# A hybrid attention block on one core: merged tiles split eight units after turning, an early table load, and a larger scratch for GpSimd's DMAs

## The chip, the core and the metric

The kernel runs on one core of a Trainium2 chip. The core has five engines with a queue each: TensorE (PE, matmuls; PEld is its weight loads), VectorE (DVE), ScalarE (ACT), GpSimd (POOL) and SyncE (SP, which here only issues DMAs). Each engine works through its own instructions in the order in which the program wrote them, and waits on semaphores for the others. The metric is device time of one execution in microseconds. The kernel before takes 912.95 us, the median of three runs (914.67, 907.07 and 912.95). Durations below come from one more execution, the profiled one: 913.56 us, of which 911.8 us are the span from the first to the last instruction.

## What is computed

One layer of a decoder block on 256 tokens of width 2048, in float32. The projections, cut to what matters here:

```python
h = rmsnorm(x, norm_w)
proj = h @ w_in            # u_pool, g_pool, q, kc_raw, vc_raw, k_sel, v_sel, k_win, v_win, g_nsa, g_br
y_pool = pool_mixer(u_pool, pool_mix, pool_scale) * silu(g_pool)
y_a = y_pool @ w_pool_out
# q, k with rope; compressed, selected and window attention, added with gates sigmoid(g_br)
y_b = (o_nsa * silu(g_nsa)) @ w_nsa_out
gm = sigmoid(h @ w_merge + b_merge).reshape(b, s, 2, D_MODEL)
merged = gm[:, :, 0] * y_a + gm[:, :, 1] * y_b
x = x + merged @ w_out
return rmsnorm(x, final_norm_w)
```

## The kernel before, in words

**Units.** The weights are cut into 314 units, in the order of `plan()`: `p` (pool inputs and gates of the branches, 420 or 416 columns), `mix`, `kc`, `vc`, `ks`, `kw`, `vs`, `vw` and the compression weights `w1k`, `w1v`, then four times `q`, `gn`, `m`, `po` (one for each group of four heads, called head 0 to 3 here), then `m4`, `m5`, `no0`, `no1`, `m6`, `no2`, `m7`, `no3` and `wo0` to `wo3`. Most are a chunk of eight units, each of 256 rows by 512 columns. The tile names carry the unit's number: `w260` is the raw weight, `h260` and `l260` its two parts.

**Three matmuls for one.** A float32 product is made of three matmuls in a rounded type: the high part `h` of the weight by the high part of the activations (L227), the low part `l` by the high part (L228), and `h` by the low part (L229). So every unit is loaded by SP, copied to `h` by ScalarE (L214), and VectorE subtracts `l = w - h` (L215). A unit is twelve matmuls: two blocks of 128 rows, two blocks of tokens, three products.

**The loop.** At step `s` the main loop writes the load of unit `s+6` (`load`), the split of unit `s+3` (`cut`), the matmuls of unit `s`, and then `advance()`, which takes one piece of work from each of five lanes (`e`, `a`, `c`, `d`, `b`). A lane is a queue of generators: the next generator begins only when the one before has ended, and each `yield` is one step. This is what sets the order of everything beside the weights. An engine may run ahead of TensorE, but not out of its own order.

**Turning.** Activations have to lie transposed for the next product. `turn` does this in lane `a` in two parts: VectorE transposes 32x32 blocks of both token blocks into `r` (STREAM_TRANSPOSE, L275, one for each token block, called the first and the second transpose here), and GpSimd then writes `r` to DRAM with one DMA (`W`, L280) and reads it back in four DMAs (L284), which put the blocks in place. The result is then split by ScalarE (`mh`, `qh`) and VectorE (`ml`, `ql`), after `TURN` = 4 further steps for `q` and for the merged tiles `m0`, `m1`, `m2` (the last, `m3`, is turned by TensorE), and after eight for `ks` and `kw`. The gates `gn` and `gp` are turned but not split.

**Merged tiles.** When chunk `no` `i` is done, `evac_no` multiplies it by its gate (VectorE, `gm`, L862), GpSimd adds it to `merged` (`mg`, L863), and `merge_t(i)` turns and splits it. The results are needed only by `wo`.

**Attention.** When `qT` of a head group is split, two generators `attend` follow in lane `b`: scores in PSUM (`S`, two buffers), added to a mask by VectorE (L702), the maxima (`mx`, L708 to L713), the exponentials by ScalarE (L723, with a load of its function table ahead of them where another function ran before), the weights, and the transposes by TensorE.

**The start.** Eight matmuls on zeros (`warm`) run while the first loads come. `x_piece(0)` brings in the first part of `x` in two halves, beside the two halves of unit 0; `cut(0)` makes unit 0's `h` on VectorE (L1078), half by half, with the parts `xh` (ScalarE, L217) and `xl` (VectorE, L218) of `x` in between.

Of the kernel before, what the change touches and what calls it, by code (L numbers as in the profile page):

```python
# [11 lines left out]
F32 = mybir.dt.float32  # L12
F32R = mybir.dt.float32r
BF16 = mybir.dt.bfloat16
AF = mybir.ActivationFunctionType
OP = mybir.AluOpType
# [172 lines left out]
def body(nc, tc, d, out):  # L189
# [7 lines left out]
    def blk(dt, name):  # L197
        return sb.tile([128, NB], dt, tag="B", bufs=NBLK, name=name)

    def half(dt, name):  # L200
        return sb.tile([128, 512], dt, tag="H", bufs=NHALF, name=name)
# [4 lines left out]
    def psum(tag, name):  # L206
        return pp.tile([128, 512], F32, tag=tag, bufs={"P": 4, "S": 2, "T": 2}[tag], name=name)

    mm, act, dve, pool = nc.tensor.matmul, nc.scalar.activation, nc.vector, nc.gpsimd

    def split(hi, lo, src, scale=None, eng=None):

        if scale is None:
            act(hi, src, AF.Copy)  # L214
            (eng or dve).tensor_tensor(lo, src, hi.bitcast(F32), op=OP.subtract)  # L215
        else:
            act(hi, src, AF.Copy, scale=scale)  # L217
            dve.scalar_tensor_tensor(lo, src, scale, hi.bitcast(F32), op0=OP.mult, op1=OP.subtract)  # L218
# [16 lines left out]
    def C(name):  # L235
        a, b = CONST[name]
        return ct[:, a:b]
# [32 lines left out]
    def turn(name, srcs, dst):  # L270


        r = blk(F32, name + "R")
        for tok, src in enumerate(srcs):
            dve.transpose(r[:, tok * 512:tok * 512 + 512].rearrange("p (b h j) -> p h b j", b=4, h=4),  # L275
                          src.rearrange("p (h b j) -> p h b j", h=4, b=4))
        yield

        w = dp.tile([128, 1024], F32, tag="W", bufs=NTURN, name=name + "W")
        pool.dma_start(w, r[:, :1024])  # L280
        wv = w.rearrange("(a i) (k b x) -> b i k a x", a=4, k=2, b=4)
        dv = dst[:, :1024].rearrange("p (k a x) -> p k a x", k=2, a=4)
        for b in range(4):
            pool.dma_start(dv[32 * b:32 * b + 32], wv[b])  # L284

    def by_head(g):

        return g[:, :1024].rearrange("p (c h j) -> p h c j", h=4, j=32)
# [4 lines left out]
    def x_piece(j):  # L293
        st = half(F32, f"xs{j}")
        if j == 0:

            nc.scalar.dma_start(nw, nwt)
            nc.scalar.dma_start(st[:, :256], xT[j][:, :256])
            unit_load(0, 0)
            nc.sync.dma_start(st[:, 256:], xT[j][:, 256:])  # L300
            unit_load(0, 1)
        else:
            nc.sync.dma_start(st, xT[j])
        if j % 2 == 0:
            xh.append(blk(F32R, f"xh{j}"))
            xl.append(blk(F32R, f"xl{j}"))
        return st

    def x_split(j, st, k):
        kt = 2 * j + k  # L310
        o = (kt % 4) * 256
        split(xh[kt // 4][:, o:o + 256], xl[kt // 4][:, o:o + 256], st[:, k * 256:k * 256 + 256],
              scale=nw[:, kt:kt + 1])
# [8 lines left out]
    def x_square(j, st):  # L322

        if j == 0:
            pool.memset(ones, 1.0)
            act(sq, st, AF.Square)
        else:
            act(st, st, AF.Square)
            pool.tensor_tensor(sq, sq, st, op=OP.add)

    def warm():

        z = half(BF16, "zero")
        dve.memset(z, 0.0)
        ps = psum("T", "warm")
        for _ in range(NWARM):
            mm(ps, z[:, :128], z, start=True, stop=True)
# [63 lines left out]
    def pool_load():  # L401
        bt.extend(blk(F32, f"bt{k}") for k in range(3))
        for k, w in enumerate((1024, 512, 1024)):
            nc.sync.dma_start(bt[k][:, :w], bic[k][:, :w])
# [35 lines left out]
    def pool_mix():  # L440
        yield
        for k in range(2):
            gpT.append(blk(F32, f"gpT{k}"))
            yield from turn(f"gp{k}", [gpn[tok][:, k * 512:k * 512 + 512] for tok in range(2)], gpT[k])
            yield
# [171 lines left out]
    def keys(kind, b, rot):  # L617
        yield
        g = blk(F32, f"{kind}T")
        yield from turn(kind, rot, g)  # L620
        for _ in range(2 * TURN):
            yield

        runs = [[KTt[h][:, z + 16 + b * 128:z + 400 + b * 128] for z in (0, 528)] for h in range(4)]
        split4([[runs_of(t) for t in pair] for pair in runs],
               [by_head(g)[:, h].rearrange("p (k a) j -> p k a j", k=2) for h in range(4)])
# [24 lines left out]
    def queries(i, rot):  # L651
        yield
        qTt[i] = (blk(F32R, f"qh{i}"), blk(F32R, f"ql{i}"))
        g = blk(F32, f"qT{i}")
        yield from turn(f"q{i}", rot, g)
        for _ in range(TURN):
            yield
        split(*(x[:, :1024].rearrange("p (h c j) -> p h c j", h=4, j=32) for x in qTt[i]), by_head(g))
        for pr in range(2):
            later("b", attend(i, pr))  # L660
# [196 lines left out]
    def evac_no(i, ps):  # L857
        g = gm.pop(4 + i)
        for tok in range(2):
            t = g[:, tok * 512:tok * 512 + 512]  # L860
            m = merged[tok, i // 2][:, (i % 2) * 512:(i % 2) * 512 + 512]
            dve.tensor_tensor(t, ps[tok], t, op=OP.mult)  # L862
            pool.tensor_tensor(m, m, t, op=OP.add)  # L863
            if tok == 0:
                yield
        later("a", merge_t(i))

    def merge_t(i):
        yield
        mh.append(blk(F32R, f"mh{i}"))  # L870
        ml.append(blk(F32R, f"ml{i}"))
        o = (i % 2) * 512
        if i == 3:

            for tok in range(2):
                pt = psum("T", f"mT{i}{tok}")
                for h in range(4):
                    nc.tensor.transpose(pt[:, h * 128:h * 128 + 128],
                                        merged[tok, 1][:, o + h * 128:o + h * 128 + 128], C("ident"))
                split(*(x[i][:, :1024].rearrange("p (h t) -> p h t", h=4)[:, :, tok * 128:tok * 128 + 128]  # L880
                        for x in (mh, ml)), pt.rearrange("p (h t) -> p h t", h=4))
                if tok == 0:
                    yield
            return
        g = blk(F32, f"mT{i}")
        yield from turn(f"m{i}", [merged[tok, i // 2][:, o:o + 512] for tok in range(2)], g)
        for _ in range(TURN):
            yield
        split(*(x[i][:, :1024].rearrange("p (h c j) -> p h c j", h=4, j=32) for x in (mh, ml)), by_head(g))

# [155 lines left out]
    def unit_load(s, k=None):  # L1046
        u = units[s]
        if s not in raw:
            raw[s] = blk(F32, f"w{s}")
        c = slice(0, u.n) if k is None else slice(k * u.n // 2, (k + 1) * u.n // 2)  # L1050
        nc.sync.dma_start(raw[s][:, c], wts[u.off:u.off + 128 * u.n].rearrange("(p n) -> p n", p=128)[:, c])

    def load(s):
        if s >= N:
            return
        if s < 16 and s % 2 == 0:
            xst[s] = x_piece(s // 2)
        if s:
            unit_load(s)
        if s == 24:  # L1060
            nc.sync.dma_start(ct, cst)
        if s == 18:
            pool_load()
        if units[s].pre:
            units[s].pre(units[s].i)

    def cut(s):
        if s >= N:
            return
        u = units[s]  # L1070
        h, l = blk(F32R, f"h{s}"), blk(F32R, f"l{s}")
        r = raw.pop(s)
        n = u.n // 2
        st = xst.pop(s, None)
        if s == 0:
            for k in range(2):
                o = slice(k * n, k * n + n)
                dve.tensor_copy(h[:, o], r[:, o])  # L1078
                x_split(0, st, k)
                dve.tensor_tensor(l[:, o], r[:, o], h[:, o].bitcast(F32), op=OP.subtract)  # L1080
        else:
            if st is not None:
                for k in range(2):
                    x_split(s // 2, st, k)
            split(h[:, :u.n], l[:, :u.n], r[:, :u.n])
        if s % 2 and s < 16:
            x_square(s // 2, xsq.pop())
        if st is not None:
            xsq.append(st)
        hl[s] = (h, l)  # L1090


    warm()
    loaded = cutted = 0
    for s in range(N):
# [27 lines left out]
TURN = 4  # L1123
# [2 lines left out]


def build():
    nc = bacc.Bacc("TRN2", target_bir_lowering=False, num_devices=1, dynamic_dma_scratch_size=1024)
    return nc  # L1130


# [35 lines left out]
```

## Time and profile before

| | |
|---|---|
| runs | 914.67, 907.07, 912.95 us; median 912.95 |
| profiled execution | 913.56 us, span 911.8 us |
| TensorE busy (modelled) | 892.4 us, 98% of the span |
| TensorE weight loads | 751.0 us, 82% |
| VectorE | 590.2 us, 65% |
| ScalarE | 461.9 us, 51% |
| GpSimd | 155.9 us, 17% |
| moved by DMA | 189.02 MB, 207 GB/s over the span |
| chain that ended last, by engine | PE 88%, DMA 4%, issue 3%, ACT 2%, DVE 2%, POOL 1% |

Reading: the ends of matmuls are modelled, so the busy time of TensorE says whether it had work, not how fast it was. How fast it was is read from the starts of neighbouring matmuls, from the count of matmuls in a stretch, and from the granted clock.

### The profile page before, as it was taken

To read this page: it belongs to the slowest core of one execution; us is meant where nothing else is said; L and a number is where in the kernel's file an instruction comes from. 1 tells how busy PE (TensorE), PEld (TensorE's weight loads), DVE (VectorE), ACT (ScalarE), POOL (GpSimd) and SP (SyncE) were. 2 spreads that over 40 slices of the span, in tenths; PEclk is the share of its full clock that TensorE was granted. 3 is DMA by queue.
4 is the path that set the end of the run, shared out by engine and by line. 5 is a ranking of instruction groups with operands and counts; after the bars stand their busy time and mean duration, and the time that the engine had idled before them with its cause. 6 is when DMAs were issued, how large, how long until landed. Compare 5 with 4: busy or idle time off the path is not lost.

```text
span 911.8 us, 11860 instructions
## 1 busy us (share of the span) xinstructions
PE 892.4 (98%) x4289; PEld 751.0 (82%) x4289; DVE 590.2 (65%) x889; ACT 461.9 (51%) x723; POOL 155.9 (17%) x145
## 2 busy tenths in 40 slices
PE   8999999999999999999999999999999979999996
PEld 7999988888888888887888888878888858888886
DVE  7756457877846476867686868576774526357633
ACT  6566545635634366456646655576562315246510
POOL 2203226333002110201021102010002311111110
PEclk9999999999999999999999999999999999999998
DMA  9955686788875664575556655666576674696602
GB/s 346 382 160 177 228 248 190 232 271 256 287 224 181 204 181 150 188 208 180 168 187 216 183 159 179 205 193 204 167 243 198 190 236 152 206 381 213 225 1 92
DMA packets 56154, 189.02 MB, mean 207 GB/s; under 512 B 6944, under 2 KB 7456, under 8 KB 56096
## 3 DMA queue, kind: packets, MB, share of 16 engines
q1 hardware_dynamic: 50768, 172.40, 58.8%
q0 software_dynamic: 5040, 15.73, 5.7%
q8 instruction: 33, 0.54, 0.2%
q14 instruction: 25, 0.20, 0.1%
q10 hardware_dynamic: 288, 0.14, 0.1%
HBM read 178.29 MB, written 9.96 MB: 206 GB/s over the span
## 4 chain that ended last, share of the span: by engine, by line
PE 88%; DMA 4%; issue 3%; ACT 2%; DVE 2%; POOL 1%; ACTq 0%; DVEq 0%; POOLq 0%
PE m L228 5%; PE m L229 5%; PE m L227 5%; PE p L227 3%; PE p L228 3%; PE p L229 3%; PE q L228 3%; PE wo L228 3%; PE wo L227 3%; PE wo L229 3%; PE q L229 3%; PE q L227 3%; PE gn L228 3%; PE gn L229 3%; PE gn L227 3%; PE no L228 3%
## 5 line engine op out<-in xcount | busy, mean ns | idle before, releaser
L215 DVE TENSOR_TENSOR l<-w,h 128x1024 fp32r<-128x1024 f32 (+2 forms) x313 | 386.0, 1262 | 80.6 <-ACT h L214 79.3
L214 ACT ACTIVATE h<-w 128x1024 fp32r<-128x1024 f32 (+2 forms) x313 | 308.2, 1030 | 56.5 <-DVE l L215 15.6
L227 PE MATMUL m<-h,xh 128*128 128x512 f32 x256 | 101.2, 395 | 0.0
L229 PE MATMUL m<-h,xl 128*128 128x512 f32 x256 | 100.8, 394 | 0.0
L228 PE MATMUL m<-l,xh 128*128 128x512 f32 x256 | 100.8, 394 | 0.0
L227 PE MATMUL p<-h,xh 128*128 128x420 f32 (+1 forms) x160 | 57.6, 360 | 1.4 <-ACT xh L217 1.4
L228 PE MATMUL p<-l,xh 128*128 128x420 f32 (+1 forms) x160 | 57.1, 357 | 0.6 <-DVE l L1080 0.6
L229 PE MATMUL p<-h,xl 128*128 128x420 f32 (+1 forms) x160 | 57.2, 357 | 0.0
L229 PEld LDWEIGHTS m<-h,xl 128*128 128x128 f32 x256 | 48.0, 188 | 11.1
L227 PEld LDWEIGHTS m<-h,xh 128*128 128x128 f32 x256 | 48.3, 189 | 9.9
L228 PEld LDWEIGHTS m<-l,xh 128*128 128x128 f32 x256 | 48.1, 188 | 9.8
L227 PE MATMUL no<-h,yh 128*128 128x512 f32 x128 | 51.6, 403 | 4.5 <-ACT h L214 4.5
L723 ACT ACTIVATE S<-S,mx 128x16 f32<-128x16 f32 (+2 forms) x96 | 37.7, 394 | 35.7 <-DVE mx L713 35.7
L227 PE MATMUL wo<-h,mh 128*128 128x512 f32 (+1 forms) x144 | 53.2, 369 | 0.0
L228 PE MATMUL wo<-l,mh 128*128 128x512 f32 (+1 forms) x144 | 53.1, 369 | 0.0
L229 PE MATMUL wo<-h,ml 128*128 128x512 f32 (+1 forms) x144 | 53.0, 368 | 0.0
L228 PE MATMUL no<-l,yh 128*128 128x512 f32 x128 | 51.5, 402 | 0.7 <-DVE l L215 0.7
L227 PE MATMUL gn<-h,xh 128*128 128x512 f32 x128 | 51.6, 403 | 0.0
L229 PE MATMUL no<-h,yl 128*128 128x512 f32 x128 | 51.4, 401 | 0.0
L227 PE MATMUL q<-h,xh 128*128 128x512 f32 x128 | 51.0, 398 | 0.0
L229 PE MATMUL gn<-h,xl 128*128 128x512 f32 x128 | 50.5, 395 | 0.0
L228 PE MATMUL q<-l,xh 128*128 128x512 f32 x128 | 50.5, 394 | 0.0
(336 smaller groups left out, 1768.6 us busy)
## 6 DMA issues: line engine op xcount, KB each, us to landing
w<-wts SPq DMA_DIRECT2D x274, 512.0 KB, 4.3
w<-wts SPq DMA_DIRECT2D x31, 420.0 KB, 7.3
w<-wts SPq DMA_DIRECT2D x8, 416.0 KB, 3.3
bb<-bmr SPq DMA_DIRECT2D x8, 256.0 KB, 4.9
xr<-xn SPq DMA_DIRECT2D x4, 512.0 KB, 6.8
out<-ot SPq DMA_DIRECT2D x8, 256.0 KB, 2.5
xs<-xT SPq DMA_DIRECT2D x7, 256.0 KB, 7.3
bt<-bic SPq DMA_DIRECT2D x2, 512.0 KB, 9.0
```

Of the source, the lines that this page charges most:

```text
L214: act(hi, src, AF.Copy)
L215: (eng or dve).tensor_tensor(lo, src, hi.bitcast(F32), op=OP.subtract)
L227: mm(o, ah, bh, start=start, stop=False)
L228: mm(o, ah, bl, start=False, stop=False)
L229: mm(o, al, bh, start=False, stop=stop)
L723: act(s, s, AF.Exp, bias=mx[:, k:k + 1], scale=SCALE, accum_out=sm[:, k:k + 1])
```

## The change

Five edits, all in the order of work:

1. `merge_t` waits `2 * TURN` = 8 steps between the turn and the split of the merged tiles, instead of 4.
2. In `turn`, the `yield` stands between the two transposes; the second transpose and the DMAs are written in the same step. The number of steps is the same. This holds for every turn (`gp`, `ks`, `kw`, `q`, `gn`, `m`).
3. ScalarE runs a one-element copy in `x_piece(0)` right behind its two DMA issues.
4. Units 0 and 1 are loaded in halves and split in halves; apart from the first half of unit 0, ScalarE makes their `h`. VectorE subtracts unit 0's first `l` before it makes `xl`.
5. The scratch memory of GpSimd's DMAs is 2048 instead of 1024.

```diff
         for tok, src in enumerate(srcs):
             dve.transpose(r[:, tok * 512:tok * 512 + 512].rearrange("p (b h j) -> p h b j", b=4, h=4),
                           src.rearrange("p (h b j) -> p h b j", h=4, b=4))
-        yield
+            if tok == 0:
+                yield
@@ x_piece(0)
             nc.scalar.dma_start(st[:, :256], xT[j][:, :256])
+
+            act(small(1, "tab"), zeros[0][:, :1], AF.Copy)
             unit_load(0, 0)
             nc.sync.dma_start(st[:, 256:], xT[j][:, 256:])
             unit_load(0, 1)
+            unit_load(1, 0)
+            unit_load(1, 1)
@@ merge_t
-        for _ in range(TURN):
+        for _ in range(2 * TURN):
             yield
@@ load
-        if s:
+        if s > 1:
             unit_load(s)
@@ cut
-        if s == 0:
+        if s < 2:
+
             for k in range(2):
                 o = slice(k * n, k * n + n)
-                dve.tensor_copy(h[:, o], r[:, o])
-                x_split(0, st, k)
-                dve.tensor_tensor(l[:, o], r[:, o], h[:, o].bitcast(F32), op=OP.subtract)
+                if s == 0 and k == 0:
+                    dve.tensor_copy(h[:, o], r[:, o])
+                else:
+                    act(h[:, o], r[:, o], AF.Copy)
+                if s == 0 and k == 0:
+                    dve.tensor_tensor(l[:, o], r[:, o], h[:, o].bitcast(F32), op=OP.subtract)
+                    for x in range(2):
+                        x_split(0, st, x)
+                else:
+                    dve.tensor_tensor(l[:, o], r[:, o], h[:, o].bitcast(F32), op=OP.subtract)
@@ build
-    nc = bacc.Bacc("TRN2", target_bir_lowering=False, num_devices=1, dynamic_dma_scratch_size=1024)
+    nc = bacc.Bacc("TRN2", target_bir_lowering=False, num_devices=1, dynamic_dma_scratch_size=2048)
```

What stands in the queues at three places. First ScalarE's queue at the start of the program, before (`xs` is a piece of `x`, `sq` its squares, `h` and `w` a unit):

```order
L298 DMA xs_93<-xT 128x256
L217 ACT_TABLE_LOAD
L217 ACTIVATE xh_100<-xs_93,nw 128x256 x2
L214 ACTIVATE h_132<-w_102 128x840
L326 ACTIVATE sq<-xs_93 128x512
```

and of the change:

```order
L299 DMA xs_93<-xT 128x256
L301 ACT_TABLE_LOAD
L301 ACTIVATE tab<-zero 128x1
L217 ACTIVATE xh_105<-xs_93,nw 128x256 x2
L1090 ACTIVATE h_125<-w_98 128x420
L1090 ACTIVATE h_135<-w_102 128x420 x2
L331 ACTIVATE sq<-xs_93 128x512
```

The table load now stands ahead of the copy `tab`, which needs no load, and the second half of unit 0 and both halves of unit 1 are ScalarE's. Second, ScalarE's queue around the split `mh1` of the second merged tile, before:

```order
L214 ACTIVATE h259_6583<-w259_6527 128x1024
L214 ACTIVATE mh1_6497<-mT1_6499 128x1024
L214 ACTIVATE h260_6603<-w260_6545 128x1024
L214 ACTIVATE h261_6623<-w261_6563 128x1024
L214 ACTIVATE h262_6644<-w262_6581 128x1024
```

and of the change:

```order
L214 ACTIVATE h265_6704<-w265_6645 128x1024
L214 ACTIVATE h266_6722<-w266_6664 128x1024
L214 ACTIVATE mh1_6556<-mT1_6558 128x1024
L214 ACTIVATE h267_6742<-w267_6682 128x1024
L214 ACTIVATE h268_6760<-w268_6700 128x1024
```

`mh1` moved from ahead of `h260` to ahead of `h267`, `mh0` from ahead of `h252` to ahead of `h256`, `mh2` from ahead of `h276` to ahead of `h280`. Because lane `a` is served in order, `merge_t(1)` begins only after `mh0`: VectorE's first transpose of `m1` now stands behind `l255`, `ml0`, `l256` and `l257` too, its second behind `l258`. Third, VectorE's queue at the turn of `q1` (`P`, `sm`, `Cn` and `S` belong to the attention of head group 0), before:

```order
L275 STREAM_TRANSPOSE q1R<-q1r0a 128x4x4x32
L275 STREAM_TRANSPOSE q1R<-q1r1a 128x4x4x32
L215 TENSOR_TENSOR P_3220<-p_3484,P_3220 128x2x128
L734 TENSOR_TENSOR sm_3365<-sm_3365,ct 128x1
L735 RECIPROCAL sm_3365<-sm_3365 128x6
L736 TENSOR_TENSOR sm_3365<-sm_3365,gates 128x6
L738 TENSOR_SCALAR Cn_3217<-S_3328,sm_3365 128x3x16
```

and of the change, up to the second transpose:

```order
L275 STREAM_TRANSPOSE q1R<-q1r0a 128x4x4x32
L215 TENSOR_TENSOR P_3225<-p_3488,P_3225 128x2x128
L742 TENSOR_TENSOR sm_3370<-sm_3370,ct 128x1
L743 RECIPROCAL sm_3370<-sm_3370 128x6
L744 TENSOR_TENSOR sm_3370<-sm_3370,gates 128x6
L746 TENSOR_SCALAR Cn_3222<-S_3333,sm_3370 128x3x16
L750 TENSOR_SCALAR S_3333<-S_3333,sm_3370 128x128 x2
L746 TENSOR_SCALAR Cn_3222<-S_3333,sm_3370 128x3x16
L750 TENSOR_SCALAR S_3333<-S_3333,sm_3370 128x2x128 x2
L215 TENSOR_TENSOR l_3505<-w_3408,h_3504 128x1024
L275 STREAM_TRANSPOSE q1R<-q1r1a 128x4x4x32
```

The second transpose of `q1`, and with it GpSimd's five DMAs, moved behind ten instructions; `q2` and `q3` read the same, at `q0` only one `l` lies between. The second transpose of `gn1` moved from ahead of the maxima `mx` to behind them and the next `l`.

## Rows read from the trace of the kernel before

**Rows 1.** Busy time by stretch: span part, engines busy (count), granted clock, DMA

```profile
core 0: us, PE busy (x) PEld busy (x) DVE busy (x) ACT busy (x) POOL busy (x), PEclk, DMA share, GB/s
0.00:20.00 20.00, 16.82 (x68) 13.68 (x69) 13.99 (x20) 13.63 (x23) 4.29 (x8) 0.91 0.92 339
...
400.00:420.00 20.00, 18.68 (x94) 15.48 (x93) 14.05 (x27) 13.03 (x32) 4.59 (x6) 1.00 0.76 237
...
580.00:600.00 20.00, 18.26 (x96) 15.15 (x95) 13.82 (x22) 13.96 (x25) 2.39 (x4) 1.00 0.72 220
...
740.00:760.00 20.00, 14.81 (x52) 11.20 (x52) 11.13 (x11) 11.11 (x12) 0.59 (x1) 0.83 0.40 129
...
780.00:800.00 20.00, 20.00 (x88) 16.28 (x87) 6.12 (x7) 4.79 (x5) 2.41 (x4) 1.00 0.68 199
```

**Rows 2.** Waits of TensorE: us in total, times, longest

```profile
PE no L227 <- ACT h L214: 4.5, 1, 4.5
PE S L227 <- DVE S L702: 3.1, 3, 1.5
PE p L227 <- ACT xh L217: 1.4, 1, 1.4
```

**Rows 3.** Timeline of the start: start, us, engine, line, operation [idle before <- releaser]

```profile
4.30 1.28 ACT L217 ACT_TABLE_LOAD   x1 [4.30 <-DMA xs<-xT]
...
6.16 0.46 PE L227 MATMUL p<-h,xh 128*128 128x420 f32 x1 [1.41 <-ACT xh L217]
...
7.04 0.37 DVE L1078 CAST h<-w 128x420 fp32r<-128x420 f32 x1
...
10.67 1.98 DVE L215 TENSOR_TENSOR l<-w,h 128x840 fp32r<-128x840 f32 x2 [0.28 <-ACT h L214]
...
13.24 0.35 PE L227 MATMUL p<-h,xh 128*128 128x420 f32 x1
```

**Rows 4.** Timeline, TensorE and ScalarE at the splits mh1 and mh2

```profile
743.97 0.40 PE L229 MATMUL no<-h,yl 128*128 128x512 f32 x1
...
746.85 1.06 ACT L214 ACTIVATE mh<-mT 128x1024 fp32r<-128x1024 f32 x1 [19.49 <-DMA mT<-m1W]
...
748.90 0.79 PE L227 MATMUL no<-h,yh 128*128 128x512 f32 x1 [4.53 <-ACT h L214]
...
755.58 0.39 PE L228 MATMUL no<-l,yh 128*128 128x512 f32 x1
...
793.17 1.06 ACT L214 ACTIVATE mh<-mT 128x1024 fp32r<-128x1024 f32 x1 [16.19 <-DMA mT<-m2W]
```

**Rows 5.** GpSimd's timeline at two turns, and all its reads back

```profile
386.44 1.82 POOL L284 DMA_DIRECT2D qT<-q1W  x3 [5.21 <-ACT h L214]
392.33 0.59 POOL L284 DMA_DIRECT2D qT<-q1W  x1 [4.07 <-issue]
...
735.66 1.82 POOL L284 DMA_DIRECT2D mT<-m1W  x3 [9.65 <-DMA m1W<-m1R]
741.63 0.59 POOL L284 DMA_DIRECT2D mT<-m1W  x1 [4.16 <-issue]
...
DMA to landing us min/median/max: 2.6/4.9/7.9
```

**Rows 6.** Timeline of VectorE and ScalarE from the turn of q1 to head 1

```profile
379.68 0.66 DVE L275 STREAM_TRANSPOSE q1R<-q1r1a 128x512 f32<-128x512 f32 x1
...
382.41 2.35 DVE L215 TENSOR_TENSOR l<-w,h 128x1024 fp32r<-128x1024 f32 x2
...
396.90 1.06 ACT L214 ACTIVATE qh<-qT 128x1024 fp32r<-128x1024 f32 x1 [4.01 <-DMA qT<-q1W]
...
405.56 1.30 DVE L275 STREAM_TRANSPOSE gn1R<-gn 128x512 f32<-128x512 f32 x2
...
409.05 1.28 ACT L723 ACT_TABLE_LOAD   x1 [0.96 <-DVE mx L713]
```

**Rows 7.** Busy time while q1 is read back, columns as in rows 1

```profile
392.00:396.00 4.00, 4.00 (x19) 3.27 (x18) 1.67 (x2) 0.88 (x1) 0.59 (x1) 1.00 0.81 212
```

## What the change will do to the time: a prediction

> **What bounds the kernel now.** I read the busy time by stretch first. TensorE has work all the time in almost every 20 us; a usual stretch holds 88 matmuls, 0.23 us from start to start (20 us / 88). Four stretches fall short: the start, 400 to 420, 580 to 600, and 740 to 760, where only 52 matmuls stand and the granted clock is 0.83 [rows 1]. So the end is set by TensorE, and time is won only where TensorE itself stands still or runs at the lower clock. Its waits then say for whom: once 4.5 us for a weight's high part `h`, three times (3.1 us together, at most 1.5) for VectorE's `S`, once 1.4 us at the start for `xh` [rows 2]. Each edit is judged by these places.
>
> **Edit 1, the later split of merged tiles.** At 746.85 ScalarE starts `mh1` after 19.49 us of standing idle for the read back of `m1`; `h260` is queued behind it, and TensorE, which has started its last matmul at 743.97, gets its next only at 748.90 [rows 4]. The wait costs more than its 4.5 us: from the matmul at 743.97 to the one at 755.58 there are 14 steps [rows 4]; at 0.23 us they take 3.2 us, and they took 11.6. The loss is 8.4 us, waits and half clock together (the clock of 0.83 over 20 us is 3.4 us of it [rows 1]).
>
> In the new order `mh1` stands ahead of `h267`. Without the stall TensorE comes to `h260` at 744.2 and, at twelve matmuls of 0.23 us a unit (2.76 us), to `h267` at 763.5. When is `m1` back? VectorE's transposes of `m1` come behind at most five more instructions of about 1.2 us (two `l` take 2.35 us [rows 6]), so `mh1` could start at 746.85 + 6.0 = 752.9 at the latest of what I can name, 10 us ahead of need. `mh2` must be ready for `h280`, at 744.2 + 20 x 2.76 = 799.4; before it started at 793.17 [rows 4], and its chain starts 8.4 us earlier, with TensorE's. `mh0` only gains room. So the wait has somewhere to go: ScalarE still idles, but with `h` for units ahead already made. **-8.4 us**; bounds 0 (the wait is only moved) and -8.4.
>
> **Edits 3 and 4, the start.** The first real matmul starts at 6.16, after `xh`, which waited for a table load of 1.28 us that ScalarE began only when its data was there, at 4.30 [rows 3]. Until then ScalarE does nothing but issue two DMAs, so a load put there is covered, and `xh` and the matmul come 1.28 us earlier. For the second half of unit 0, VectorE's copy at 7.04 was queued, not waiting for data [rows 3]; ScalarE now makes it beside VectorE's `l`. I do not know when its load lands, only that it is before 7.04. Unit 2's first matmul started at 13.24, while the first of two `l` of the pair that begins at 10.67 is unit 2's and ends near 11.7 [rows 3]. So TensorE can be at most about 13.24 - 11.7 + 0.2 = 1.7 us early there (the second matmul needs `l`). Below: the granted clock over the first 20 us is 0.91 [rows 1], that is 3.6 us at half speed; if that stretch stays where it is, a start 1.28 us earlier is worth half, 0.6 us. **-1.3 us**, between -0.6 and -1.7; 1.3 because both first matmul and unit 0's second half move by it. The cover is there as long as the load of `x` takes until 4.30; the loads behind the extra issue may come a little later, and `l` of unit 2, ready 1.7 us ahead of its use before, hides that.
>
> The Trainium skill (ScalarE: Activation LUTs, section "What ACT_TABLE_LOAD costs") puts a table switch at about 2.66 us, load and drain. The row shows 1.28 us and `xh` soon behind it; by the page this term would be -2.7 and the whole 902.5. The row decides.
>
> **Edit 5, the larger scratch.** In each turn GpSimd issues three of its four reads back to back (1.82 us) and then stands for some time before the fourth: 4.07 us at `q1`, 4.16 at `m1`, with no releaser ("issue") [rows 5]. I take this as waiting for room for descriptors, which the doubled scratch gives; no row names it. What it is worth is not 4 us, as the data has to move: landing takes 2.6 to 7.9 us, median 4.9 [rows 5]. The fourth of `q1` was issued at 392.33 and let ScalarE go at 396.90 [rows 5, 6]. Issued with the others it would land with the third, and the third's slowest landing, 387.7 + 7.9, is 395.6: 1.3 us earlier at the least if the ring was the limit, and up to 3.8 us (median landing, 392.6 + 0.5). Between 392 and 396 the DMA engines were 0.81 busy [rows 7]; if they are the limit, nothing is won.
>
> **Edit 2, the second transpose a step later.** At `q1` it ended at 380.34; behind it came `P` and the `sm` group until 382.41, then `l147`, half of 2.35 us [rows 6]. In the new order these go first: about 2.1 + 1.2 = 3.3 us later, and so all five DMAs of GpSimd. Behind `qh` on ScalarE stand the next `h`, `gn` and the exponentials, and for those TensorE waits at `S`. For a head that is 3.3 us late and 1.3 to 3.8 us early again; also, once the turn starts later, it runs beside fewer weight loads. So `qT` lands between 0.5 us earlier and 3.3 us later (nothing won by edit 5). I take 0.6 later, near the middle of the two cases with a working ring. Against it stands the relief for which the `yield` moved: `gn1`'s two transposes took 1.30 us right ahead of the maxima, for which ScalarE waited at 409.05 [rows 6]; one of them now comes behind: -0.65. Per head that makes 0. Only two stretches show loss there (400 to 420: 1.3 us, 580 to 600: 1.7 us [rows 1]), heads 1 and 3, so no more than 3.0 us can be won. **0 us**, between -3.0 and 2 x (3.3 - 0.65) = +5.3. At `gp`, `ks`, `kw` and `q0` TensorE waits for nothing now [rows 2], and there the ring alone is felt.
>
> **The sum.** 911.8 - 8.4 - 1.3 + 0 = 902.1 us of span. The profiled execution lay 1.76 us above its span (913.56 - 911.8): **903.9 us**. The median of the runs, 912.95, is 0.6 us below the profiled execution; one run, 907.07, was 6 us faster than the others, as if the long wait had been shorter in it. About 1% is what a measurement of this kernel can tell from no change; against the median that is 903.8 and 922.1, and the forecast lies on the first bound.
>
> **The rivals.**
> *The heads win too.* The ring gives more than the late transpose takes, and the waits at heads 1 and 3 go: 903.9 - 3.0 = 900.9. For it: 4 us of GpSimd's waits are larger than 3.3. Against: 0.81 busy DMA engines.
> *The heads lose.* `qT` lands late by 1.7 us (the third's landing, 395.6, plus 3.3, against 396.9 is 2.0; less for fewer loads). The waits grow by 1.05 us each, and a wait of 2.5 us and more may draw the lower clock, as that of 4.5 us did; it cost 3.4 us there. 903.9 + 2.1 + 3.4 = 909.4 with one such stretch.
> *The ring does nothing.* DMA engines, not room for descriptors, set the landing. The heads are 2.65 us later each: 903.9 + 5.3 = 909.2. The Trainium skill (DMA: Bandwidth & Descriptors, "Issuing engines are not separate DMA queues") says that all queues run on the same 16 DMA engines and interleave, which speaks for this one; the busy share of 0.81 agrees.
> *The wait at the merged tiles only moves.* Then the change does not do what it says: 903.9 + 8.4 = 912.3. Against it: 10 us of room.
> *Slower.* One mechanism: `qT` comes later than 3.3 us, since the turn falls among other weight loads (landings of 7.9 us instead of 4.9). The wait grows at heads 1, 2 and 3, each drawing the lower clock, 3.4 us. With L the lateness of `qT`, that costs 3 x (L - 0.65) + 10.2. It is no gain any more (9.7 us) as soon as all three draw the clock, and over 1% slower (18.2 us above the forecast) from L = 3.3 on; at 3.5 it gives 922.7. For it: the clock did fall once in this trace; against: waits of 1.5 us did not draw it (1.00 in both stretches [rows 1]).
>
> **Chances and range.** Forecast 0.50, on the bound, half of it beyond: 0.25 faster, 0.25 same; its own range is 902.0 to 906.0. Heads win 0.21, faster. Heads lose 0.11, same. Ring does nothing 0.07, same. Wait only moves 0.07, same. Slower 0.04. Together faster 0.46, same 0.50, slower 0.04. The range of 8 in 10 leaves out the slow rival, the moved wait and the outer parts of the heads that win: 899.8 to 909.5.
>
> **What would show it.** Right: near 744 TensorE steps from unit to unit, the clock stays 1.00 from 740 to 760, and 20 us hold 88 matmuls; the first real matmul is at 4.9; the fourth read of each turn follows the third within 0.7 us. Wrong: TensorE waits for an `h` behind `mh1` or `mh2`; the waits for `S` grow beyond 3.1 us in sum, or one at head 2 is added; the fourth read still stands apart. The forecast falls if `qT` lands more than 2 us later than now, or if the start is held by the landing of unit 0's second half.

## The result, and the profile after

The changed kernel takes 901.28 us, the median of four runs (899.8 to 901.77), against 910.92 us for the kernel before beside it (four runs, 907.07 to 914.67): a ratio of 0.989, 95% interval 0.984 to 0.994. It is 1.1% faster. A second measurement (six runs beside eleven) gave 900.59 against 910.1 us, 0.990 (0.988 to 0.993). The forecast was 903.9 us, its range 899.8 to 909.5: 2.6 us too high, inside the range. The profiled execution took 899.8 us, its span 898.0 us.

Busy time by stretch after the change (columns as in [rows 1]):

```profile
0.00:20.00 20.00, 18.27 (x79) 14.57 (x80) 14.49 (x21) 15.08 (x26) 4.52 (x8) 1.00 0.91 334
400.00:420.00 20.00, 20.00 (x93) 16.52 (x92) 17.63 (x34) 13.08 (x33) 4.72 (x6) 1.00 0.70 195
580.00:600.00 20.00, 20.00 (x95) 16.45 (x95) 16.34 (x32) 12.65 (x33) 4.30 (x6) 1.00 0.70 203
740.00:760.00 20.00, 20.00 (x88) 16.29 (x87) 10.64 (x12) 7.46 (x8) 4.00 (x2) 1.00 0.64 220
```

All four short stretches of [rows 1] are full or nearly so: 740 to 760 holds 88 matmuls instead of 52, and the granted clock is 1.00 there and at the start. TensorE's waits (us in total, times, longest), beside that for the zeros of the warm-up:

```profile
PE p L227 <- ACT h L1090: 0.3, 1, 0.3
PE p L228 <- DVE l L1096: 0.2, 1, 0.2
```

The waits for `h` behind `mh1` and for `S` [rows 2] are gone. For a sum by stretch I took each time between the starts of neighbouring matmuls and subtracted the median for that shape (0.232 us for 512 columns). Before, the loss so counted is 4.0 us in the first 20 us, 1.6 at 400, 2.3 at 580 and 8.3 at 740; after, 1.9 at the start and nothing elsewhere. That is 14.2 us (summed before rounding), against 13.8 us of span (911.8 - 898.0).

The start (timeline; ScalarE and TensorE):

```profile
1.66 1.28 ACT L301 ACT_TABLE_LOAD   x1 [1.66 <-PEq L1145]
2.96 0.20 ACT L301 ACTIVATE tab<-zero 128x1 f32<-128x1 bf16 x1
4.84 0.72 PE L227 MATMUL p<-h,xh 128*128 128x420 f32 x1
11.00 0.35 PE L227 MATMUL p<-h,xh 128*128 128x420 f32 x1
```

The table load lies under the loads of `x`; the first real matmul is at 4.84 instead of 6.16 and unit 2's first, the last row, at 11.00 instead of 13.24 [rows 3].

GpSimd's reads back of `q1` and `m1`, the counterpart of [rows 5]:

```profile
387.26 2.42 POOL L285 DMA_DIRECT2D qT<-q1W  x4 [4.60 <-ACT h L214]
732.57 2.43 POOL L285 DMA_DIRECT2D mT<-m1W  x4 [8.85 <-DMA m1W<-m1R]
```

Four reads in one row, where before the fourth stood alone about 4 us later. It is so in all 15 turns. The traces also tell what the fourth read had waited for, though the row names no releaser: in each of the 60 turns of the four traces with a scratch of 1024 it is issued 0.33 us after the turn's first read landed. At `q1` before, that read was issued at 386.44 and landed at 392.00; the fourth was issued at 392.33 [rows 5].

The stretch from `gn1`'s transpose to head 1's exponentials (VectorE, then ScalarE), the counterpart of the last rows of [rows 6]:

```profile
402.76 0.70 DVE L275 STREAM_TRANSPOSE gn1R<-gn 128x512 f32<-128x512 f32 x1
404.72 1.28 ACT L731 ACT_TABLE_LOAD   x1
406.02 0.31 ACT L731 ACTIVATE S<-S,mx 128x16 f32<-128x16 f32 x1
```

From the transpose to the first exponential it is 3.26 us now. Before it was 4.79 us (405.56 to 410.35). Two things shortened it: one transpose instead of two stands ahead of the maxima (0.6 us), and the table load has no releaser any more, where it had waited 0.96 us for `mx` (0.9 us). At head 3, the other one where TensorE had stood still, the load still waits, and the same stretch went only from 4.79 to 4.19 us:

```profile
586.14 1.28 ACT L731 ACT_TABLE_LOAD   x1 [0.95 <-DVE mx L721]
```

The semaphores in the traces say when the load waits. In the 14 traces (before, after and the twelve runs below) 112 table loads stand ahead of exponentials. The load waits for VectorE exactly where the first exponential behind it waits for another semaphore (ScalarE's own at head 1 before, TensorE's at head 3 after). Where the exponential itself waits for VectorE, the load does not. Why edit 2 changes which semaphore the exponential waits for was not followed.

ScalarE's three merged splits, the counterpart of [rows 4]:

```profile
711.99 1.06 ACT L214 ACTIVATE mh<-mT 128x1024 fp32r<-128x1024 f32 x1 [5.20 <-DMA mT<-m0W]
742.06 1.06 ACT L214 ACTIVATE mh<-mT 128x1024 fp32r<-128x1024 f32 x1 [1.58 <-DMA mT<-m1W]
781.88 1.04 ACT L214 ACTIVATE mh<-mT 128x1024 fp32r<-128x1024 f32 x1
```

ScalarE stands idle ahead of `mh1` for 1.58 us instead of 19.49. `h267`, which is queued behind it, ends at 744.07; TensorE comes to it at 758.45.

### The profile page after: what moved, and what is told of

Its sections match the earlier page's. It is cut to its first block, busy times and chain, and to the rows that moved or that the text cites. A ratio compares the mean times of both kernels' runs of the same rounds, so it can differ in the third digit from the quotient of the medians.

```text
span 898.0 us, 11882 instructions
## 1 busy us (share of the span) xinstructions
PE 888.4 (99%) x4289; PEld 748.0 (83%) x4289; DVE 593.7 (66%) x889; ACT 464.0 (52%) x726; POOL 156.7 (17%) x145
## 4 chain that ended last, share of the span: by engine, by line
PE 98%; DMA 1%; DVE 0%; ACT 0%; SPq 0%; issue 0%; DVEq 0%; ACTq 0%
PE m L229 7%; PE m L228 7%; PE m L227 7%; PE p L228 3%; PE p L227 3%; PE p L229 3%; PE wo L229 3%; PE gn L229 3%; PE gn L228 3%; PE q L228 3%; PE q L229 3%; PE wo L227 3%; PE no L228 3%; PE wo L228 3%; PE gn L227 3%; PE no L227 3%
## 5 line engine op out<-in xcount | busy, mean ns | idle before, releaser
L229 PE MATMUL q<-h,xl 128*128 128x512 f32 x128 | 50.4, 394 | 0.0
L228 PE MATMUL gn<-l,xh 128*128 128x512 f32 x128 | 50.4, 394 | 0.0
```

Of the source, the lines that this page charges most:

```text
L228: mm(o, ah, bl, start=False, stop=False)
L229: mm(o, al, bh, start=False, stop=stop)
```

## The experiments

The trace after the change could be read as three gains that add up: 8.3 us at the merged split, 3.8 us at heads 1 and 3, 2.1 us at the start. I tried this by doing parts alone and by undoing parts. Each group of four ran on one chip, beside runs of the kernel before:

| edits in the kernel | median us | kernel before beside it | ratio (95% interval) | TensorE's waits apart from the start, us: for `S`; others |
|---|---|---|---|---|
| 1 | 903.76 | 910.16 | 0.993 (0.991 to 0.996) | 2.1 |
| 5 | 905.48 | 910.16 | 0.995 (0.994 to 0.997) | 2.4 |
| 2 | 921.62 | 910.16 | 1.013 (1.010 to 1.017) | 2.8; `no` 6.6, `vs`, `vw` 3.4 |
| 2, 5 | 903.29 | 910.16 | 0.993 (0.990 to 0.995) | 0.2; `vs` 0.2 |
| 2, 3, 4, 5 | 902.07 | 909.53 | 0.991 (0.989 to 0.994) | 0.2; `no` 1.0 |
| 1, 3, 4, 5 | 904.82 | 909.53 | 0.995 (0.992 to 0.997) | 4.3 |
| 1, 2, 3, 4 | 909.62 | 909.53 | 1.001 (0.999 to 1.003) | 4.3; `ql`, `qh` 1.2, `vs`, `vw` 2.2 |
| 1, 2, 5 | 904.33 | 909.53 | 0.994 (0.992 to 0.996) | 2.1 |
| 1 to 5 | 900.59 | 910.1 | 0.990 (0.988 to 0.993) | 0.5; `vs` 0.5 |
| 1, 2, 4, 5 | 902.04 | 910.1 | 0.992 (0.990 to 0.994) | 1.0 |
| 1, 2, 3, 5 | 902.09 | 910.1 | 0.992 (0.990 to 0.995) | 0.7 |
| 1 to 5, scratch 1536 | 901.43 | 910.1 | 0.991 (0.989 to 0.994) | 1.1 |

### Edit 1 alone

```diff
-        for _ in range(TURN):
+        for _ in range(2 * TURN):
             yield
         split(*(x[i][:, :1024]...
```

> The kernel before with edit 1 alone (2*TURN steps ahead of the merged split); nothing else is changed. Theory (three gains that add up: merged split 8.3 us, heads 1 and 3 3.8 us, start 2.1 us of the 13.8 us of span): the wait for h behind mh1 is gone, no half clock near 750, span 911.8 - 8.3 = 903.5 us, ratio 0.991; the waits for S stay at about 3 us in sum, and the fourth read of each turn still stands about 4 us behind the third. Rival (the scratch is needed for it: with the small scratch m1 comes back too late even for h267): TensorE waits for an h again near 763, 1 to 3 us, span 905 to 908 us.

903.76 us, span 902.1 us. TensorE's waits:

```profile
PE S L227 <- DVE S L702: 2.1, 2, 1.4
PE p L227 <- ACT xh L217: 1.4, 1, 1.4
```

No wait for `h`, 88 matmuls between 740 and 760, clock 1.00 there. The wait does not move to `h267`, and the larger scratch is not needed for it; the rival fell. But the medians differ by 6.4 us, not 8.3: the profiled execution of before (913.56 us) lay 3.4 us above the median of these 15 runs (906.09 to 914.07). What varies among those runs was not profiled; their mean granted clock runs from 0.998 (906.09 us) down to 0.991, the value of the profiled execution, so that the length of the half-clock stretches is part of it.

### Edit 5 alone

```diff
-    nc = bacc.Bacc("TRN2", ..., dynamic_dma_scratch_size=1024)
+    nc = bacc.Bacc("TRN2", ..., dynamic_dma_scratch_size=2048)
```

> The kernel before with edit 5 alone (scratch 2048). Theory: the fourth read follows within 0.7 us in every turn, the turned tile lands 1.3 to 3.8 us earlier; the heads lose their waits for S (-3.8 us), and the wait for h260 behind mh1 shrinks from 4.5 us to between 0.7 and 3.2 us, perhaps without the low clock: together -5 to -11 us, span 901 to 907 us. Rival (the fourth read is early only because edit 2 lays the turn among fewer loads; the scratch does nothing): the fourth read still waits for about 4 us, span 911 to 912 us.

905.48 us, span 903.9 us. From the timeline, GpSimd at `q1` and ScalarE at `mh1` and at head 1; then TensorE's wait for `S`:

```profile
386.71 2.43 POOL L284 DMA_DIRECT2D qT<-q1W  x4 [5.58 <-DMA q1W<-q1R]
738.14 1.06 ACT L214 ACTIVATE mh<-mT 128x1024 fp32r<-128x1024 f32 x1 [12.20 <-DMA mT<-m1W]
408.69 1.28 ACT L723 ACT_TABLE_LOAD   x1 [0.96 <-DVE mx L713]
```

```profile
PE S L227 <- DVE S L702: 2.4, 2, 2.2
```

The four reads go back to back, so the scratch does set the fourth read's time. `mh1` starts 8.7 us earlier than before (746.85) and nobody waits for it: with this edit alone the stall at the merged tile is gone too. Of the 8.7 us, 6.0 are the write of `m1`, which landed at 728.89 instead of 734.91: it was issued 1.4 us earlier and took 4.9 us instead of 9.5. Over the 14 traces this write took 4.9 to 9.5 us, so these two are the ends of its range, and no run shows that the scratch had a part in that. At the heads the theory fell. The fourth read of `q1` was issued 3.87 us earlier (388.46 against 392.33), but landed at 396.36 instead of 396.74; issued together, the last two took 8.0 and 7.9 us. The wait at head 1 is there as before, with the same wait of the table load for `mx`. The granted clock behind that wait of 2.2 us (416 to 422 us) was 0.72, so the stretch from 400 to 420 lost 3.6 us here.

### Edit 2 alone

```diff
         for tok, src in enumerate(srcs):
             dve.transpose(...)
-        yield
+            if tok == 0:
+                yield
```

> The kernel before with edit 2 alone (yield between the two transposes, scratch 1024). Theory (the scratch makes the heads' gain, the later transpose costs): the fourth read still waits for about 4 us, qT lands 1 to 3 us later relative to TensorE, the waits for S grow from 3.1 to between 4 and 8 us, and mh1 starts about 1 to 2.4 us later, so the wait behind it grows from 4.5 to 5.5 to 7 us: span 914 to 920 us. Rival (the later transpose itself makes the heads' gain, as the reads then fall among fewer loads): waits for S under 1 us, span 908 to 911 us.

921.62 us, 1.3% slower. TensorE's waits, and from the timeline ScalarE's split of the turned `ks`:

```profile
PE no L227 <- ACT h L214: 4.7, 1, 4.7
PE S L227 <- DVE S L703: 2.8, 3, 1.4
PE vs L228 <- DVE l L215: 1.4, 2, 0.8
PE vw L227 <- ACT h L214: 1.0, 1, 1.0
```

```profile
209.07 1.34 ACT L222 ACTIVATE KT<-ksT 128x256 fp32r<-128x256 f32 x4 [13.71 <-DMA ksT<-ksW]
```

The waits at `mh1` came as expected, those for `S` did not grow in sum. New are the waits at `vs` and `vw`, which I had not thought of: the split of `ks` starts at 209.07, where it started at 202.78 before, and the `h` and `l` of units of `vs` stand behind it. In `ks`'s turn the write took 7.2 us (5.9 before) and the first three reads 6.8 to 8.2 us (3.7 to 4.2), and the fourth still had to wait: the later turn fell among slower transfers there.

### Edits 2 and 5 together

The two diffs above in one kernel.

> The kernel before with edits 2 and 5 together (later second transpose, scratch 2048). Theory (edit 2 gives little or nothing of its own at the heads): waits for S gone as with the scratch alone (-3.8 us), the wait behind mh1 between 1 and 5 us, span 903 to 909 us, at most 2 us off the scratch alone, on the slower side. Rival (the heads need both edits): only here the waits for S vanish, and with either alone they stay above 2 us in sum.

903.29 us, span 899.2 us. From the timeline, VectorE and ScalarE at `gn1` and head 1; then TensorE's wait for `S`:

```profile
404.70 0.71 DVE L275 STREAM_TRANSPOSE gn1R<-gn 128x512 f32<-128x512 f32 x1
406.67 1.28 ACT L724 ACT_TABLE_LOAD   x1
407.96 0.31 ACT L724 ACTIVATE S<-S,mx 128x16 f32<-128x16 f32 x1
```

```profile
PE S L227 <- DVE S L703: 0.2, 1, 0.2
```

The rival held in these four traces: only with both edits do the waits for `S` vanish. The heads differ, though. With edit 2 alone head 1 has no wait left; the 2.8 us stand at head 2 (500.9) and head 3 (591.9, 602.5). From the transposes of `gn1` to the first exponential it is 3.26 us here, as in the changed kernel, and 4.79 us with the scratch alone (405.19 to 409.98 in that trace). So what edit 2 gives head 1 is at `gn1`, not at `qT`. I did not know that the table load would lose its wait with it; the order of ScalarE's instructions there is the same, and what differs is the semaphore that the exponential waits for.

### The changed kernel without edit 1

```diff
-        for _ in range(2 * TURN):
+        for _ in range(TURN):
```

> The changed kernel with edit 1 undone (the merged split TURN steps behind the turn again). Scratch alone brought the merged tile back 8.7 us earlier (738.03 against 746.74) and left no wait at mh1. Theory now (edits 1 and 5 each suffice; their gains do not add): no wait for an h behind mh1, span 898 to 899 us and time 900.5 to 902.5 us, no difference from the changed kernel. Rival (edit 1 carries 8.3 us of its own, as predicted): the wait behind mh1 is back, 3 us or more, time 905 to 910 us.

902.07 us. From the timeline, ScalarE at `mh1`, and TensorE behind it:

```profile
737.49 1.06 ACT L214 ACTIVATE mh<-mT 128x1024 fp32r<-128x1024 f32 x1 [15.42 <-DMA mT<-m1W]
741.00 0.50 PE L228 MATMUL no<-l,yh 128*128 128x512 f32 x1 [0.95 <-DVE l L215]
```

Nearly as the theory had it: TensorE waits 1.0 us for `l260` and 0.15 us for `h260`, and loses 1.5 us in all where the kernel before lost 8.3. Edits 1 and 5 each take away most of the same stall; edit 1 alone adds room (14 us between `h267` and its use, instead of none at `h260`).

### The changed kernel without edit 2

```diff
             dve.transpose(...)
-            if tok == 0:
-                yield
+        yield
```

> The changed kernel with edit 2 undone (both transposes ahead of the yield), scratch 2048. Theory (edit 2 gives the heads about 3 us once the scratch is large, because the maxima of head 1 start earlier): a wait for S of 1 to 2.5 us at head 1 and under 1 us at head 3, time 902.5 to 904.5 us. Rival (edit 2 is worth nothing beside the scratch and the start): waits for S under 0.5 us, time 900.5 to 902 us.

904.82 us, just above what was expected (902.5 to 904.5), as are both waits; its 12 runs spread from 899.22 to 909.08. ScalarE's table load at head 1, from the timeline, and TensorE's wait for `S`:

```profile
406.69 1.28 ACT L730 ACT_TABLE_LOAD   x1 [0.96 <-DVE mx L720]
```

```profile
PE S L227 <- DVE S L709: 4.3, 2, 2.7
```

The table load waits for `mx` again, and TensorE waits 2.7 us at head 1 and 1.5 us at head 3.

### The changed kernel without edit 5

```diff
-    nc = bacc.Bacc("TRN2", ..., dynamic_dma_scratch_size=2048)
+    nc = bacc.Bacc("TRN2", ..., dynamic_dma_scratch_size=1024)
```

> The changed kernel with edit 5 undone (scratch 1024). Theory (edit 2 costs without the scratch, at the turns of ks and kw and at head 2 as well): TensorE waits 2 to 5 us in sum at vs and vw, 2 to 4 us at S, none behind mh1 (edit 1), fourth reads about 4 us apart: time 905 to 912 us. Rival (the early start or edit 1 also clears these): time under 903 us.

909.62 us, ratio 1.001 (0.999 to 1.003): without the scratch the other four edits together give nothing. GpSimd's fourth read of `q1`, from the timeline, and three of TensorE's waits:

```profile
395.40 0.59 POOL L285 DMA_DIRECT2D qT<-q1W  x1 [2.37 <-issue]
```

```profile
PE S L227 <- DVE S L710: 4.3, 4, 1.4
PE vs L228 <- DVE l L215: 1.4, 2, 0.8
PE vw L228 <- DVE l L215: 0.8, 1, 0.8
```

The fourth read stands apart again, the waits at `vs` and `vw` are back as with edit 2 alone (2.2 us against 3.4), and there is none behind `mh1`, as edit 1 is in.

### The changed kernel without edits 3 and 4

```diff
@@ x_piece(0)
-            act(small(1, "tab"), zeros[0][:, :1], AF.Copy)
...
-            unit_load(1, 0)
-            unit_load(1, 1)
@@ cut
-        if s < 2:
+        if s == 0:
...
```

> The changed kernel with edits 3 and 4 undone (start as before). Theory (the start is worth 2.1 us, 1.3 of it the table load, the rest in units 1 and 2): time 902.5 to 904 us, first real matmul at 6.1. Rival (the start only sets the clock: the gain is there only where the half clock near 8 us fell away, and then it is small): time within 0.7 us of the changed kernel, 900.8 to 902.2.

904.33 us, just above the theory's range. ScalarE's split of `q1`, from the timeline, and TensorE's waits:

```profile
399.06 1.06 ACT L214 ACTIVATE qh<-qT 128x1024 fp32r<-128x1024 f32 x1 [5.76 <-DMA qT<-q1W]
```

```profile
PE S L227 <- DVE S L703: 2.1, 2, 1.3
PE p L227 <- ACT xh L217: 1.5, 1, 1.5
```

Beside the start it has 2.1 us of waits for `S`, which the kernel with edits 2 and 5 alone, the same at the heads, did not have. In this execution the reads of `q1` took 6.4 to 6.7 us and let `qh` go 20.5 us after TensorE's first matmul of unit 144 (378.61); there it was 18.9 us. Why transfers at 390 us should be slower here is not settled. So what lies between this ratio and that of the changed kernel, 0.990, is not the start's alone.

### The changed kernel again, and without edit 3, without edit 4, with a scratch of 1536

> The changed kernel once more, as the measure for the three runs beside it on the same chip. Expected by every theory: 900 to 902.5 us, TensorE waits for nothing but 1 us at the start.

900.59 us, with waits of 0.5 us for `S` and 0.5 us at `vs`.

```diff
-            act(small(1, "tab"), zeros[0][:, :1], AF.Copy)
```

> The changed kernel with edit 3 undone (no copy ahead, so the table load stands ahead of xh again), halves kept. Theory (the table load is the main term of the start, 1.3 of 2.1 to 3 us): first real matmul at 6.1, a wait of 1.3 us for xh, time 1.0 to 1.5 us above the changed kernel on the same chip. Rival (the start is held by the loads of units 0 to 2, so the time only moves into the wait for the second half of unit 0): within 0.5 us of the changed kernel, with unit 2's first matmul still at 11.0.

902.04 us, 1.45 us above the changed kernel, as the theory had it. From the timeline of TensorE, the first and the twenty-fifth real matmul (unit 2's first):

```profile
6.07 0.46 PE L227 MATMUL p<-h,xh 128*128 128x420 f32 x1 [1.28 <-ACT xh L217]
10.89 0.36 PE L227 MATMUL p<-h,xh 128*128 128x420 f32 x1
```

But in the trace the rival held: the first matmul is 1.2 us later, but unit 2 begins at 10.89, no later than with the early load (11.00). What TensorE gains ahead with the early load it loses again at unit 0's second half, which begins at 7.02 there with two waits and at 7.46 here with none.

Edit 4 undone, the copy `tab` kept:

```diff
@@ x_piece(0)
-            unit_load(1, 0)
-            unit_load(1, 1)
@@ cut
-        if s < 2:
+        if s == 0:
...
```

> The changed kernel with edit 4 undone (units 0 and 1 whole or split by VectorE as before), the early table load kept. Theory: first real matmul at 4.8, but the stretch at half clock from about 8 us stays, and unit 2's first matmul is at 12 to 12.5 (13.24 before, 11.00 with both edits): time 0.8 to 1.5 us above the changed kernel. Rival (the early table load makes the whole gain): within 0.4 us of the changed kernel, no half clock.

902.09 us, 1.5 us above the changed kernel. From the timeline of TensorE, the second real matmul:

```profile
5.83 0.46 PE L228 MATMUL p<-l,xh 128*128 128x420 f32 x1 [0.47 <-DVE l L1085]
```

The first is at 4.80, but `l` comes late, and unit 2's first matmul is at 11.56. Unit 3's is at 15.52 before, 13.84 here, 13.31 without edit 3 and 13.49 with both edits: with either of them nearly the whole of it is there. There is no stretch at half clock in either trace, which was the rival's sign. So the times came out as the theories had them, the traces as the rivals; the intervals of the ratios overlap with the changed kernel's, the starts do not explain 1.5 us, and I leave it open.

```diff
-    nc = bacc.Bacc("TRN2", ..., dynamic_dma_scratch_size=2048)
+    nc = bacc.Bacc("TRN2", ..., dynamic_dma_scratch_size=1536)
```

> The changed kernel with a scratch of 1536 instead of 2048. Theory (the fourth read waited for room for its descriptors: 1024 hold three reads, so 1536 hold four): the fourth read follows within 0.7 us, time as the changed kernel within 1 us. Rival (what helps is not room for a fourth read but something that comes only with the doubled size): the fourth read stands 3 to 5 us apart again, waits at vs, vw and S, time 905 to 910 us as without the larger scratch.

901.43 us, the same as the changed kernel as far as this tells. GpSimd's reads of `q1`, from the timeline:

```profile
387.32 2.42 POOL L285 DMA_DIRECT2D qT<-q1W  x4 [4.21 <-ACT h L214]
```

Half the added scratch is enough for the four reads to go back to back. So it is room, as predicted.

## Where the prediction was right, and where not

**The base.** The sum was made against the profiled execution of 913.56 us. The median of before is 910.92 us in the runs beside the changed kernel, 2.6 us lower; the profiled execution of the changed kernel was 1.5 us below its median. Between the two executions 13.8 us went, of which the sum had 9.7; between the medians 9.6 us went. So the 2.6 us by which the forecast was high are the base, and the gain of 9.7 us fits the medians. That fit is luck: as the terms below show, edit 1 was counted too high, the heads and the start too low.

**Edit 1, -8.4 us.** Right: the trace lost 8.3 us at 740 and keeps none of it; `mh1` started at 742.06, ahead of the 752.9 given as the latest. The rival of a wait that only moves fell in the kernel with edit 1 alone. The half clock near 750 went with the stall. Two things were missing. Over the runs the term is 6.4 us (edit 1 alone). And it is no term of edit 1 only: with the scratch alone the stall was gone as well. The prediction priced the earlier fourth read at `q1` and never asked what it does at `m1`, where its own rows showed the same gap (4.16 us).

**Edit 5, room for descriptors.** Right in its mechanism: 1536 is enough, 1024 is not. And the rows could have named it: the fourth read follows the landing of the turn's first read by 0.33 us in every turn with a scratch of 1024. Wrong in the price at `q1`: 1.3 to 3.8 us earlier was forecast, 0.38 us was measured with the scratch alone. The lower bound rested on the third read's slowest landing, 7.9 us; of the four reads issued together the last three took 7.4 to 8.0 us. The Trainium skill (DMA: Bandwidth & Descriptors, "Issuing engines are not separate DMA queues") says that DMAs run on the same 16 engines and interleave whoever issued them; the 0.38 us at `q1` agrees with it. At the other turns of `q` the price was about right. From the first read's issue to the last landing, the two traces with the larger scratch and without edit 2 are shorter than the two with the small scratch and without edit 2 by 2.7 us at `q0`, 0.3 at `q1`, 2.5 at `q2`, 1.2 at `q3` and 1.4 at `m1` (means of two). At `m1` the tile came 8.7 us earlier with the scratch alone, but 6.0 us of that were there when the write landed (728.89 against 734.91), and no run here shows why the write was faster.

**Edit 2, 0 us at the heads.** The lateness of the turn was right: counted from TensorE's first matmul of unit 144 (378.15 before, 376.28 after), the write of `q1` is issued 5.79 us behind instead of 2.50, 3.3 us later. The step from there to `qT` came out near, but by another sum: 0.6 us later was taken. The fourth read lands 18.6 us behind that matmul before, 17.7 after, and between 17.7 and 20.3 in the eight profiled kernels that have edits 2 and 5, 18.8 on average: 0.2 us later. It was not the ring that made up for the 3.3 us, as the forecast had it. With edit 2 alone, on the small scratch, the fourth read lands 18.3 us behind (19.9 in the changed kernel without edit 5). The reads lie among fewer weight loads, which the prediction named and priced at nothing beyond the middle: without edit 2 they are issued from 8.3 to 8.7 us behind, with two loads of weights on their way and a third issued at 9.1, and take 9.7 to 10.3 us together; with it they are issued from 10.7 to 12.0 us behind, when one or two loads are on their way, and take 6.7 to 8.6.

What failed is the relief at `gn1`: 0.65 us, one transpose. At head 3 it is that, 0.6 us. At head 1 it was 1.5 us, as the table load of 1.28 us ahead of the exponentials no longer waits for the maxima but runs beside them. In the four kernels traced without edit 2 (before, and those with edits 1; 5; and 1, 3, 4, 5) that load waits 0.96 us at head 1, and TensorE waits 2.1 to 4.3 us for `S` in all. In the eight with edits 2 and 5 it does not wait, and TensorE waits 0 to 2.1 us. "The heads win too", 900.9 us, is what the profiled execution shows, through a mechanism that this rival did not have.

With edit 2 in, head 1 hangs on `qT` instead. Of the ten traces with edit 2 TensorE waits there in the three in which `qh` starts 19.7, 20.1 and 20.5 us behind the first matmul of unit 144, for 0.6, 0.9 and 1.3 us; at 17.8 to 19.2 us it does not. So the cover at head 1 is small, and slower reads use it up.

**What was hidden.** "At `gp`, `ks`, `kw` and `q0` TensorE waits for nothing now [rows 2], and there the ring alone is felt": this was wrong. Edit 2 makes `ks` late there; the split starts at 204.49 in the changed kernel, 1.7 us later than before in spite of the larger scratch, and at 207 to 209 without it, where TensorE waits. What was missing is the lead that covered this place: the split started 5.6 us ahead of TensorE's first matmul of `vs` before, 1.9 ahead after, and waits stand in the traces in which it is about 1.1 us or less. So the cover was about 4.5 us, and it is nearly used up: 0 to 0.5 us of wait at `vs` remain in the traces with both edits.

**The start, -1.3 us.** Measured 2.0 us at unit 3's first matmul and 2.1 us in the sum by stretch; at unit 2's, where the bound stood, it was 2.2, and the upper bound of 1.7 was broken. It took unit 2's `l` as fixed at 11.7, but with unit 1 in halves ScalarE and VectorE reach unit 2 earlier: its `l` ended at 11.24, and its first matmul came at 11.00. And the sum put it on the table load, while with either edit nearly all of it is there. The lower bound assumed that the half clock stays; it did not. None of the eight traces with edit 3 or 4 has a granted clock below 1.00 in the first 20 us; of the six with the start as before four have 0.91. But that is not the edits' work alone: with the start as before, the kernel with edits 2 and 5 ran its first 20 us at 1.00 and began unit 3 at 13.93 instead of 15.52. Of six such traces it is the only one that early. So most of the 2.0 us is the half clock, and beside that trace the edits give 0.1 to 0.9 us.

The Trainium skill (ScalarE: Activation LUTs, "What ACT_TABLE_LOAD costs") gives 2.66 us for a switch. Here the load took 1.28 us, and the copy behind it began 0.02 us after its end; undoing the early load moved the first matmul by 1.2 us. The row was right to decide.

**The slower side.** It was given 0.04 for this change, and the change as a whole shows none of it. Its mechanism, a turn that falls among other loads, is real: with edit 2 alone it made the kernel 1.3% slower, at `ks` and `m1` rather than at the heads.

## What to carry to other kernels

A gain counted edit by edit from one trace adds up only if the edits work at different waits: here edits 1 and 5 each take away most of the same stall, edits 2 and 5 clear the heads only together and not in every trace, and edit 2 costs 1.3% alone. When an edit delays a step that many places share, list the lead at every place, also where nothing waits now. And before pricing an earlier issue, look at what the transfer then runs beside: with the same scratch the four reads together took 0.3 us less at one turn and 2.7 us less at another.

## What the runs showed of the hardware

With a scratch of 1024 the fourth read of a turn was issued 0.33 us after the first one had landed, in all 60 turns of four traces, and so 1.1 to 6.6 us behind the end of the third's issue; with 1536 and 2048 it followed at once. A table load without a wait of its own ran beside VectorE's maxima: 0.9 of the 1.5 us by which the exponentials of head 1 came earlier, in the same order of instructions. In all 112 cases the load waited for VectorE exactly where the exponential behind it waited for another semaphore. A wait of 2.2 us at head 1 was followed by a granted clock of 0.72 over 416 to 422 us in the trace with the scratch alone, while behind the longer one of 2.7 us in the changed kernel without edit 2 it stayed at 1.00. The program as it was at the start ran with a granted clock of 0.91 over its first 20 us in four profiled executions and of 1.00 in two; in one of these two (edit 2 alone) the matmuls of 420 columns still started 0.35 us apart until 10.1 us, as they do in the half-clock stretch before, instead of 0.19.
